# A two-layer encoder: q's head norm applied as a per-partition scale in the exponentials, and weight roundings queued behind PSUM evictions

## The chip, the cores and the metric

One Trainium2 chip; the kernel runs on one core. The metric is the device time of one execution in microseconds (us). A core has a matrix engine (PE, or TensorE), three engines for elementwise work (DVE, or VectorE; ACT, or ScalarE; POOL, or GpSimd) and SP, which in this kernel issues the DMAs. Each engine has its own instruction queue; they wait for each other by semaphores. Matmul results go to PSUM, and an engine reads them from there ("evicts" them) into SBUF, where the operands lie.

## The reference

Two layers over a sequence of 512 tokens of width 1024, then a last RMS norm. Cut to what the change touches:

```python
def gqa(h):                                   # 8 query heads, 2 key/value heads, width 64
    g_q = rope(rms_norm(g_q, q_norm))         # norm over each head's 64 values, then rotary
    g_k = rope(rms_norm(g_k, k_norm))
    for block of 128 queries:
        p = softmax(g_q @ g_k.T * 64 ** -0.5)
        o = p @ g_v

for l in range(2):
    h = rms_norm(x, norm_mix[l])
    x = x + concat([neighbourhood_attention(h), gqa(h)]) @ w_out[l]
    x = x + memory_cross_attention(rms_norm(x, norm_mem_q[l]), rms_norm(mem, norm_mem_kv[l]))
    x = x + conv_ffn(rms_norm(x, norm_ffn[l]))     # up, depthwise conv, silu(gate) * value, down
return rms_norm(x, norm_final)
```

Neighbourhood attention (NA) has 8 heads of width 64 over a window of the token grid; memory attention has 4 heads of width 128 over 256 memory tokens. All data are float32.

## The kernel before

**Products in three terms.** Every operand of a matmul is split into a rounded high part and the remainder, `hi` and `lo`, and a product is the sum of hi x hi, hi x lo and lo x hi. Activations lie transposed: features on the 128 partitions, tokens along the free axis.

**Weights.** `plan` lists all weight tiles in the order of their use. `emit_raw` loads one by DMA; `emit_split` (L245) rounds it: the high part is a copy on ACT (L265), the low part a subtraction on POOL (L266), in two halves for most weights. `get_w` (L269) is called where a weight is first used, and emits the roundings of the next two at that point. There are two raw buffers and four pairs of rounded ones. Outside the FFN the roundings are given a later place by priority (`behind(W_BEHIND)`).

**Order on the engines.** PE and SP run in the order of the program. On ACT, DVE and POOL a scheduler orders by priority; `behind(n)` moves an instruction back by n places, a negative n forward. `late(n, fn)` puts a step off by n ticks of the loop, so that a chain of small steps is spread between matmuls. `weave` runs attention stages over units one after the other and calls a filler, `attn_fill`, between them, which supplies matmuls of the projections until a given amount is used up. `attn_fill.step(n)` (L1029) takes n filler steps ahead of NA's weave: 3 in layer 0, 8 in layer 1.

**PSUM.** Three kinds of tiles: `ps_mm` (4 buffers, projections and products), `ps_s` (2, attention scores), `ps_t` (2, transpositions and statistics).

**First projections.** In layer 0 `project_first` (L604) works on the first three blocks q0, k0, q1 at once, as the input arrives; `project_qk` (L630) does one block, in two halves; `project_v` the values. `split_q` (L679) and `split_k` (L661) evict a block: a high copy on ACT and a subtraction on DVE for each of two heads (L682 and L684 for q). `split_psum` (L470) is the same for other tiles (L472 ACT, L473 DVE; with a scale L475 and L476).

**GQA's q and k.** `gqa_rope` (L835) takes each of q's four groups and k through steps one or two ticks apart. At the projection's end: two ACT readings of PSUM, the gained copy (L840) and the square (L841), and DVE's product with the cosines (L842). `swap`: four DMAs exchange partitions, eight small matmuls with `pairs` sum the squares per head (L850, into a `ps_t` tile), DVE divides and adds (L852, L855). `rotate`: POOL takes the power -1/2 (L862), copies it along each head's rows (L863), and does two passes of the rotation (L864, L865). `norm`: four matmuls on the identity turn the rows into a PSUM tile; one tick on, DVE multiplies the rotated tile into it (L875), and the split reads that.

**GQA's scores and softmax.** Per layer 16 units of 128 queries and two heads (j). `gqa_scores` (L889): matmuls into two score tiles, for each j the negated row maximum on DVE (L900) and the exponential with row sums on ACT (L902); then a reciprocal (L908), a per-partition multiply on POOL (`normalise`, L479), transposition and values. `mem_scores` (L1069) is memory attention's: the row maxima of two blocks in one instruction (L1076), their product with the query norms `mq.rstd`, 128x2 by 128x2 (L1077), and two exponentials whose scale is `mq.rstd` (L1081).

**The end.** `down_last` (L1225) adds the last products into x by chunks; ACT multiplies each by the final gain (L1241), while the squares go to the statistic; L1251 on DVE and L1249 on POOL multiply by the norm, and the result is stored.

Of the kernel before, what the change touches and what calls it, by code (L numbers as in the profile page):

```python
# [18 lines left out]
P = 128  # L19
# [5 lines left out]
NB = S // P  # L25
# [27 lines left out]
W_BEHIND, N_RAW, N_W, AHEAD, AHEAD_HELD, N_WARM, N_LATE, N_FIRST = 45, 2, 4, 2, 5, 8, 4, 3  # L53
# [120 lines left out]
def encoder_kernel(ctx: ExitStack, tc: tile.TileContext, t: dict, out: bass.AP):  # L174
# [60 lines left out]

    def raw_tile():
# [13 lines left out]
    def emit_split(act=ACT, cuts=2):  # L250
# [11 lines left out]
        with behind(W_BEHIND if done[0] and key[0] not in ("up", "down") else 0):  # L262
            for i in range(cuts):
                k = slice(nk * i // cuts, nk * (i + 1) // cuts)
                act.copy(hi[:, k], raw[:, k])  # L265
                (POOL if eng[0] == "P" else DVE).tensor_sub(lo[:, k], raw[:, k], f(hi)[:, k])  # L266
# [203 lines left out]
    def split_psum(hi, lo, ps, scale=None):  # L470
        if scale is None:
            ACT.copy(hi, ps)  # L472
            DVE.tensor_sub(lo, ps, f(hi))  # L473
        else:
            ACT.mul(hi, ps, scale)  # L475
# [56 lines left out]
    mem_rep = cpool.tile([P, MEMN], F32, name="mem_rep")  # L532

# [55 lines left out]
    for l in range(DEPTH):  # L589
# [41 lines left out]
        def project_qk(n, p):  # L631
            w = get_w((n, p))
            pm = ps_mm()
# [27 lines left out]
        def split_k(pm, kt, near):  # L661
            rows = [(slice(64 * j, 64 * j + 64), slice(64 - 64 * j, 128 - 64 * j)) for j in range(2)]
            for k, (r, o) in zip(kt, rows):
                ACT.copy(k[r, 0], pm[r])
                if near:
                    ACT.copy(k[o, 0], pm[r])
# [168 lines left out]
        def gqa_rope(g, pm):  # L835

            gain = qkg[:, l, 0:1] if g != "k" else qkg[:, l, 1:2]
            xs, sq, cc = tmp(), tmp(), tmp()
            with behind(-20):
                ACT.activation(xs, pm, AF.Copy, scale=gain)  # L840
                ACT.activation(sq, pm, AF.Square)  # L841
                DVE.scalar_tensor_tensor(cc, pm, gain, gtab[0][:, 0], op0=ALU.mult, op1=ALU.mult)  # L842

            def swap():
# [3 lines left out]
                pv = ps_t()  # L848
# [9 lines left out]
            def rotate(xr, v):  # L858
                r = small(2 * NB)
                rows = tmp()  # L860
                with behind(-40):
                    POOL.tensor_tensor(r, v, mhalf[:, : 2 * NB], op=ALU.pow)  # L862
                    POOL.tensor_copy(rows.rearrange("p (b d) -> p b d", d=HD), r.unsqueeze(2).to_broadcast([P, 2 * NB, HD]))  # L863
                POOL.tensor_mul(xr, xr, gtab[0][:, 1])  # L864
                POOL.tensor_add(xr, cc, xr)  # L865
                late(2, lambda: norm(xr, rows))

            def norm(xr, rows):
# [3 lines left out]
                late(1, lambda: split(xr, pr))  # L872

            def split(xr, pr):
                DVE.tensor_mul(pr, xr, pr)  # L875
                if g == "k":
                    gk.extend(rtile((2, S)) for _ in range(2))
                    split_k(pr, gk, False)
                else:
                    gq[g] = rtile((2, S))  # L880
                    split_q(pr, gq[g])
# [6 lines left out]
        def gqa_scores(u):  # L888
# [9 lines left out]
            for j in range(2):  # L898
                c = slice(j, j + 1)
                DVE.tensor_reduce(nmx[:, c], sc[j], axis=AX.X, op=ALU.max, negate=True)  # L900
                e = tmp()
                ACT.activation(e, sc[j], AF.Exp, bias=nmx[:, c], accum_out=sums[:, c])  # L902
# [126 lines left out]
        attn_fill.step(N_FIRST if l == 0 else N_FIRST + 5)  # L1029
# [39 lines left out]
        def mem_scores(u):  # L1069
# [7 lines left out]
            DVE.tensor_mul(nmx, nmx, mq.rstd[:, 2 * bp : 2 * bp + 2])  # L1077
# [154 lines left out]
        def down_last(g):  # L1232
# [144 lines left out]
```

## Time and profile before

| | |
|---|---|
| runs | 1391.63 us median of 3 (1390.44, 1391.63, 1395.34) |
| profiled execution | 1393.77 us, of which the span of the records is 1392.0 |
| mean granted TensorE clock | 0.994 |
| NA, layer 0 (with the start) / layer 1 | 0 to 140 / 703 to 824 us |
| GQA | 140 to 240 / 824 to 922 |
| memory attention | 240 to 327 / 922 to 1009 |
| FFN | 327 to 703 / 1009 to 1392 |

The stage limits are read from the timeline and rounded to a us. In the rows of the profile, `L265 ACT CAST hi<-raw 128x512` is an instruction of line 265 on ACT that writes tile `hi` from `raw`; `x2` counts instructions that a row puts together. In timeline rows the first two numbers are the start and the time that the row covers, and the bracket is the engine's idle time ahead of it and the instruction that ended it. DVE and ACT rows show the tiles they read and write, so a row `mm<-t,mm` reads and writes a projection's PSUM buffer.

### The profile page before, as it was taken

To read this page: it belongs to the slowest core of one execution; us is meant where nothing else is said; L and a number is where in the kernel's file an instruction comes from. 1 tells how busy PE (TensorE), PEld (TensorE's weight loads), DVE (VectorE), ACT (ScalarE), POOL (GpSimd) and SP (SyncE) were. 2 spreads that over 40 slices of the span, in tenths; PEclk is the share of its full clock that TensorE was granted. 3 is DMA by queue.
4 is the path that set the end of the run, shared out by engine and by line. 5 is a ranking of instruction groups with operands and counts; after the bars stand their busy time and mean duration, and the time that the engine had idled before them with its cause. 6 is when DMAs were issued, how large, how long until landed. Compare 5 with 4: busy or idle time off the path is not lost.

```text
span 1392.0 us, 19198 instructions
## 1 busy us (share of the span) xinstructions
PE 1354.7 (97%) x7072; PEld 1157.8 (83%) x7072; DVE 834.8 (60%) x1430; ACT 711.8 (51%) x1321; POOL 719.3 (52%) x537
## 2 busy tenths in 40 slices
PE   8999899999999999999999989999999999999997
PEld 7897789877888888888888978998788888888897
DVE  6666766364787177357446556754638843871873
ACT  6676577655443134234557656766554422432453
POOL 2458776635444444444645677756264444444441
PEclk9999999999999999999999999999999999999999
DMA  7653312422333333333356523223133333333331
GB/s 214 185 145 96 87 46 66 116 63 61 98 100 103 94 91 97 101 94 94 105 147 169 139 72 95 65 71 112 40 98 97 101 91 97 98 93 106 90 93 61
DMA packets 218205, 138.83 MB, mean 100 GB/s; under 512 B 6016, under 2 KB 211072, under 8 KB 218112
## 3 DMA queue, kind: packets, MB, share of 16 engines
q1 hardware_dynamic: 217968, 137.60, 34.6%
q8 instruction: 56, 0.92, 0.3%
q14 instruction: 37, 0.30, 0.1%
q10 hardware_dynamic: 144, 0.00, 0.0%
HBM read 125.00 MB, written 2.10 MB: 91 GB/s over the span
## 4 chain that ended last, share of the span: by engine, by line
PE 89%; DVE 4%; ACT 4%; issue 1%; DMA 1%; POOL 0%; DVEq 0%; ACTq 0%; SPq 0%
PE mm L77 82%; PE sc L77 4%; PE tr L64 3%; PE tr L77 1%; ACT hi L265 1%; DVE r L473 1%; DMA raw<-in_w_in 1%; ACT t L745 1%; DVE s L900 1%; DVE s L1077 1%; DVE xg L473 0%; DVE t L842 0%; ACT t L841 0%; ACT t L840 0%; ACT xg L438 0%
## 5 line engine op out<-in xcount | busy, mean ns | idle before, releaser
L266 POOL TENSOR_TENSOR lo<-raw,hi 128x1024 fp32r<-128x1024 f32 (+2 forms) x268 | 499.0, 1874 | 496.9 <-ACT hi L265 468.9
L77 PE MATMUL mm<-xg,hi 128*128 128x512 f32 x1984 | 617.7, 393 | 3.1 <-DVE t L842 2.9
L77 PEld LDWEIGHTS mm<-xg,hi 128*128 128x128 f32 x1984 | 370.4, 189 | 78.9 <-DVE t L842 3.3
L265 ACT CAST hi<-raw 128x512 fp32r<-128x512 f32 (+2 forms) x276 | 224.6, 837 | 346.7 <-PE mm L77 292.9
L77 PE MATMUL mm<-xg,lo 128*128 128x512 f32 x992 | 387.3, 391 | 0.0
L77 PE MATMUL mm<-r,hi 128*128 128x512 f32 (+1 forms) x1144 | 331.6, 374 | 2.3 <-ACT t L444 2.2
L77 PEld LDWEIGHTS mm<-r,hi 128*128 128x128 f32 x1144 | 207.3, 188 | 39.7 <-ACT t L444 3.1
L1201 DVE SCALAR_TENSOR_TENSOR t<-t,par,t 128x7 f32<-128x7 f32 (+1 forms) x352 | 201.9, 641 | 34.0 <-ACT t L1194 34.0
L77 PEld LDWEIGHTS mm<-xg,lo 128*128 128x128 f32 x992 | 187.1, 189 | 39.6
L77 PE MATMUL mm<-r,lo 128*128 128x512 f32 (+1 forms) x572 | 213.4, 373 | 0.0
L77 PEld LDWEIGHTS mm<-r,lo 128*128 128x128 f32 x572 | 108.0, 189 | 19.0
L1186 DVE TENSOR_TENSOR t<-mm,rep 128x512 f32<-128x512 f32 x88 | 60.1, 687 | 78.2 <-PE mm L77 62.1
L479 POOL TENSOR_SCALAR t<-t,s 128x512 f32<-128x512 f32 (+1 forms) x112 | 66.3, 608 | 75.4 <-DVE s L908 35.4
L1203 ACT ACTIVATE t<-t 128x512 f32<-128x512 f32 x44 | 27.8, 633 | 134.8 <-DVE t L1201 134.7
L1207 DVE TENSOR_TENSOR r<-t,r 128x512 fp32r<-128x512 f32 x44 | 90.5, 2056 | 7.4 <-ACT r L1206 4.3
L1230 DVE TENSOR_TENSOR xT<-xT,mm 128x512 f32<-128x512 f32 x32 | 21.9, 685 | 106.8 <-PE mm L77 106.8
L64 PE MATMUL tr<-ident,t 128*128 128x128 f32 x456 | 63.2, 275 | 13.3 <-DVE r L473 3.8
L77 PE MATMUL sc<-r,r 128*128 128x256 f32 (+1 forms) x352 | 72.6, 338 | 3.5 <-DVE r L473 2.5
L64 PEld LDWEIGHTS tr<-ident,t 128*128 128x128 f32 x456 | 52.4, 141 | 22.9 <-issue 9.7
L1194 ACT ACTIVATE t<-t,par 128x512 f32<-128x512 f32 x88 | 66.8, 806 | 3.2 <-DVE t L1186 3.2
L77 PE MATMUL mm<-r,r 128*128 128x256 f32 (+1 forms) x428 | 61.8, 297 | 0.0
L77 PEld LDWEIGHTS sc<-r,r 128*128 128x128 f32 x352 | 52.1, 192 | 8.3 <-DVE r L473 3.0
(145 smaller groups left out, 1554.1 us busy)
## 6 DMA issues: line engine op xcount, KB each, us to landing
raw<-in_w_up SPq DMA_DIRECT2D x88, 512.0 KB, 3.9
raw<-in_w_in SPq DMA_DIRECT2D x33, 512.0 KB, 4.5
raw<-in_w_down SPq DMA_DIRECT2D x32, 448.0 KB, 3.9
raw<-in_w_mem_kv SPq DMA_DIRECT2D x16, 512.0 KB, 4.0
raw<-in_w_down SPq DMA_DIRECT2D x16, 512.0 KB, 4.2
r<-in_bias SPq DMA_DIRECT2D x16, 384.0 KB, 5.8
r<-r SPq DMA_DIRECT2D x22, 256.0 KB, 5.2
raw<-in_w_out SPq DMA_DIRECT2D x8, 512.0 KB, 3.8
```

The source lines that it names most:

```text
L64: return lambda *a, **k: self.tc.keep_in_program_order(op(*a, **k))
L77: return self.tc.keep_in_program_order(self.engine.matmul(out, lhsT, rhs, **k))
L265: act.copy(hi[:, k], raw[:, k])
L266: (POOL if eng[0] == "P" else DVE).tensor_sub(lo[:, k], raw[:, k], f(hi)[:, k])
L473: DVE.tensor_sub(lo, ps, f(hi))
L479: eng.tensor_scalar(e, e, sums[:, col : col + 1], 1.0, op0=ALU.mult, op1=ALU.mult)
L1186: DVE.tensor_mul(u, us[side], ffn.rep)
L1194: ACT.activation(cc, u, AF.Identity, bias=par[:, l, CB + ch : CB + ch + 1], scale=w[1])
L1201: DVE.scalar_tensor_tensor(cc[:, dst], u[:, src], wi, cc[:, dst], op0=ALU.mult, op1=ALU.add)
L1203: ACT.activation(cs[0], cs[0], AF.Silu)
L1207: DVE.tensor_sub(acts[j][1], cs[0], f(acts[j][0]))
L1230: DVE.tensor_add(xT[m], xT[m], pm)
```

## The change

- `emit_split`: outside the FFN each high copy of a weight is ordered behind the last PSUM evictions on ACT that the program has written so far. Two are remembered in `evicted`: "projection" (`split_k`, `split_q`, the square of `gqa_rope`) and "other" (`split_psum`).
- `N_FIRST` 4 in place of 3; layer 1 still takes 8 steps.
- Layer 0's first two blocks (q0, k0) use `ps_s` tiles; in layer 1 `project_qk` does so for p = 0.
- `gqa_rope`: the pair statistics go to a `ps_mm` tile. For q the power is written to a lasting tile `qr[g]`; the copy along the rows, the identity matmuls and the multiply are left out, and the split reads the rotated SBUF tile one tick after the rotation. k keeps the old way.
- `gqa_scores`: the negated maximum is multiplied by q's norm (DVE, 128x1), and the exponential's scale is that norm.
- `mem_scores`: one 128x2 multiply becomes two per-partition multiplies of 128x1.
- `down_last`: the final gain is applied on DVE.

```diff
-W_BEHIND, N_RAW, N_W, AHEAD, AHEAD_HELD, N_WARM, N_LATE, N_FIRST = 45, 2, 4, 2, 5, 8, 4, 3
+W_BEHIND, N_RAW, N_W, AHEAD, AHEAD_HELD, N_WARM, N_LATE, N_FIRST = 45, 2, 4, 2, 5, 8, 4, 4
...
-        with behind(W_BEHIND if done[0] and key[0] not in ("up", "down") else 0):
+        ffn = key[0] in ("up", "down")
+        with behind(W_BEHIND if done[0] and not ffn else 0):
             for i in range(cuts):
                 k = slice(nk * i // cuts, nk * (i + 1) // cuts)
-                act.copy(hi[:, k], raw[:, k])
+                with ExitStack() as after:
+                    for e in evicted.values() if not ffn else ():
+                        after.enter_context(tc.issue_after(e))
+                    act.copy(hi[:, k], raw[:, k])
                 (POOL if eng[0] == "P" else DVE).tensor_sub(lo[:, k], raw[:, k], f(hi)[:, k])
...
-            ACT.copy(hi, ps)
+            evicted["other"] = ACT.copy(hi, ps).ins
...
+    qr = [cpool.tile([P, 2 * NB], F32, name=f"qr{i}") for i in range(4)]
...
-                    w[u], pms[u] = get_w(NA_ORDER[u]), ps_mm()
+                    w[u], pms[u] = get_w(NA_ORDER[u]), ps_s() if u < 2 else ps_mm()
...
-            pm = ps_mm()
+            pm = ps_mm() if p else ps_s()
...
             for v, r, o in halves:
-                ACT.copy(v[r], pm[r])
+                evicted["projection"] = ACT.copy(v[r], pm[r]).ins
...
-                pv = ps_t()
+                pv = ps_mm()
...
             def rotate(xr, v):
-                r = small(2 * NB)
-                rows = tmp()
+                r = small(2 * NB) if g == "k" else qr[g]
                 with behind(-40):
                     POOL.tensor_tensor(r, v, mhalf[:, : 2 * NB], op=ALU.pow)
-                    POOL.tensor_copy(rows.rearrange("p (b d) -> p b d", d=HD), r.unsqueeze(2).to_broadcast([P, 2 * NB, HD]))
+                if g == "k":
+                    rows = tmp()
+                    with behind(-40):
+                        POOL.tensor_copy(rows.rearrange("p (b d) -> p b d", d=HD), r.unsqueeze(2).to_broadcast([P, 2 * NB, HD]))
                 POOL.tensor_mul(xr, xr, gtab[0][:, 1])
                 POOL.tensor_add(xr, cc, xr)
-                late(2, lambda: norm(xr, rows))
+                if g == "k":
+                    late(2, lambda: norm(xr, rows))
+                else:
+                    late(1, lambda: split(xr))
...
+                r = 2 * b + j
                 DVE.tensor_reduce(nmx[:, c], sc[j], axis=AX.X, op=ALU.max, negate=True)
+                normalise(nmx[:, c], qr[i], r)
                 e = tmp()
-                ACT.activation(e, sc[j], AF.Exp, bias=nmx[:, c], accum_out=sums[:, c])
+                ACT.activation(e, sc[j], AF.Exp, bias=nmx[:, c], scale=qr[i][:, r : r + 1], accum_out=sums[:, c])
...
-        attn_fill.step(N_FIRST if l == 0 else N_FIRST + 5)
+        attn_fill.step(N_FIRST if l == 0 else N_FIRST + 4)
...
-            DVE.tensor_mul(nmx, nmx, mq.rstd[:, 2 * bp : 2 * bp + 2])
+            for i in range(2):
+                normalise(nmx[:, i : i + 1], mq.rstd, 2 * bp + i)
...
-                with behind(20):
-                    ACT.activation(xc, xc, AF.Copy, scale=gfin[:, m : m + 1])
+                DVE.tensor_scalar(xc, xc, gfin[:, m : m + 1], 1.0, op0=ALU.mult, op1=ALU.mult)
```

`normalise(e, sums, col, eng=DVE)` is unchanged: a `tensor_scalar` that multiplies e by one column of `sums`, one value to each partition (L479).

More of the change, by code (lines that the diff above doesn't have):

```diff
@@ L234, in encoder_kernel @@
     done = [0]
+    evicted = {}
     def raw_tile():
@@ L663, in split_k @@
             for k, (r, o) in zip(kt, rows):
-                ACT.copy(k[r, 0], pm[r])
+                e = ACT.copy(k[r, 0], pm[r])
                 if near:
-                    ACT.copy(k[o, 0], pm[r])
+                    e = ACT.copy(k[o, 0], pm[r])
+            evicted["projection"] = e.ins
             for k, (r, o) in zip(kt, rows):
```

16 lines of the change are left out of this document (9 added, 7 removed).

## The prediction

> **What bounds the kernel now.** I read the engines' busy time first, then busy time by stage, and then the timeline of TensorE (PE) for every place where it stood idle.
>
> ```profile
> PE 1354.7 (97%) x7072; PEld 1157.8 (83%) x7072; DVE 834.8 (60%) x1430; ACT 711.8 (51%) x1321; POOL 719.3 (52%) x537
> ```
>
> PE is busy for 97% of the span and no other engine for more than 60%. So the time can shrink in two ways only: less matmul work, or shorter idle times of PE. By stage (start, end, then busy time of PE, weight loads, DVE, ACT, POOL, then granted clock, DMA share, GB/s):
>
> ```profile
> 39.00:140.00 101.00, 97.58 (x620) 87.45 (x619) 62.55 (x154) 67.10 (x162) 62.12 (x66) 1.00 0.53 144
> 140.00:240.00 100.00, 93.61 (x602) 83.11 (x601) 69.43 (x128) 69.05 (x160) 70.39 (x83) 0.98 0.23 67
> 240.00:327.00 87.00, 83.33 (x443) 70.39 (x441) 46.76 (x92) 51.75 (x106) 42.68 (x27) 1.00 0.26 74
> 327.00:703.00 376.00, 375.99 (x1670) 311.72 (x1671) 222.25 (x309) 153.15 (x208) 180.85 (x88) 1.00 0.34 100
> 824.00:922.00 98.00, 94.03 (x601) 84.40 (x601) 65.44 (x125) 68.09 (x159) 69.92 (x83) 0.97 0.24 69
> 836.00:842.00 6.00, 6.00 (x25) 5.13 (x25) 2.66 (x7) 1.78 (x5) 6.00 (x8) 0.72 0.76 224
> ```
>
> The FFN (327 to 703) is full: 375.99 of 376 us, and nothing in this change can shorten it. The first layer's neighbourhood attention (to 140), GQA (to 240) and memory attention (to 327) leave PE idle for 3.4, 6.4 and 3.7 us; the second layer runs the same stages again (its GQA is the row from 824). In the last row PE's granted clock is 0.72 on average; I come back to it.
>
> These are the idle times that the change can reach (start, duration, and in brackets PE's idle time before it and what ended it):
>
> ```profile
> 34.84 0.35 PE L77 MATMUL mm<-hi,xg 128*128 128x256 f32 x1 [1.51 <-DVE r L684]
> 120.09 0.73 PE L77 MATMUL mm<-xg,hi 128*128 128x512 f32 x2 [1.44 <-DVE t L842]
> 138.67 0.63 PE L64 MATMUL tr<-ident,t 128*128 128x128 f32 x4 [1.91 <-DVE r L473]
> 148.91 1.05 PE L77 MATMUL tr<-pairs,t 128*128 128x2 f32 x8 [1.33 <-ACT t L841]
> 163.79 0.63 PE L64 MATMUL tr<-ident,t 128*128 128x128 f32 x4 [1.68 <-POOL r L524]
> 289.29 0.70 PE L64 MATMUL tr<-ident,t 128*128 128x128 f32 x4 [0.76 <-DVE t L479]
> 305.69 0.74 PE L77 MATMUL sc<-r,r 128*128 128x256 f32 x4 [1.27 <-DVE r L473]
> 823.15 0.99 PE L64 MATMUL tr<-ident,t 128*128 128x128 f32 x4 [1.91 <-DVE r L473]
> 834.96 1.05 PE L77 MATMUL tr<-pairs,t 128*128 128x2 f32 x8 [1.33 <-ACT t L841]
> 849.83 0.63 PE L64 MATMUL tr<-ident,t 128*128 128x128 f32 x4 [1.67 <-DVE xg L473]
> ```
>
> The second layer repeats the waits of 120, 289 and 305; its first stage has none like that of 34.84.
>
> **The change part by part.** Gains are minus.
>
> *Norm matmuls on the identity.* Each q group has four, eight rows in the trace:
>
> ```profile
> 127.51 1.05 PE L77 MATMUL mm<-ident,t 128*128 128x128 f32 x8
> 128.32 0.71 PE L77 MATMUL mm<-xg,hi 128*128 128x512 f32 x2
> ```
>
> Start to start that is 0.81 us of PE. Four q groups in two layers lose it: 8 x 0.81 = 6.5. In layer 1 one of them stands ahead of the wait at 823.15, whose chain does not get shorter (q's two ACT copies take the place of a rounding), so its 0.8 is only turned into waiting. I take 7 x 0.81 = -5.7; bounds 0 (all eaten by later waits) and -6.5. POOL's copy and DVE's multiply of the same groups leave too; they are off PE's path.
>
> *Weight roundings behind evictions.*
>
> ```profile
> 117.03 1.14 ACT L265 CAST hi<-raw 128x512 fp32r<-128x512 f32 x2
> 118.07 0.70 ACT L840 ACTIVATE t<-mm,qkg 128x512 f32<-128x512 f32 x1
> 118.64 0.61 ACT L841 ACTIVATE t<-mm 128x512 f32<-128x512 f32 x1
> 119.29 0.75 DVE L842 SCALAR_TENSOR_TENSOR t<-mm,qkg,r 128x512 f32<-128x512 f32 x1 [0.78 <-ACT t L841]
> ```
>
> Two halves of a rounding (1.14) run directly ahead of L840 and L841, and DVE's L842 frees the buffer for which PE stands idle for 1.44 at 120.09. Behind the change L840 and L841 stand first, so the chain ends 1.1 earlier: -1.1 in each layer, -2.2 together; bounds 0 and -2.9. What is late next is the rounded weight. At that place it is the first out projection's: subtraction on POOL from 118.82, first use at 149.82.
>
> ```profile
> 118.82 2.51 POOL L266 TENSOR_TENSOR lo<-raw,hi 128x512 fp32r<-128x512 f32 x2
> 149.82 0.71 PE L77 MATMUL mm<-r,hi 128*128 128x512 f32 x2
> ACT hi L265 <- PE mm L77: 292.9, 104, 5.9
> ```
>
> It is done at 121.3, 28 us early. The last row (all waits of that kind: us, times, longest) says that roundings mostly wait until PE releases a weight buffer, not for ACT. So I cost the delay at nothing; without that cover it would be up to one eviction, 1.3 (L840 and L841), per weight.
>
> *Score banks for the first two blocks, and N_FIRST 4.* The wait of 1.51 at 34.84 is for one of four projection buffers, which q0's eviction (L684) held. q0 and k0 now sit in the two score banks, idle until the first scores, so I take it as gone: -1.5, bounds 0 and -1.5. The extra filler step puts the value blocks ahead of the first scores: the same matmuls in another order, 0. The pair statistics take projection buffers instead of transposition ones: ten short uses, cost 0, bound +1.5 (one wait like that of 34.84).
>
> *The turn from NA to GQA.* With one filler step more, layer 0 does not have the three transpositions at 138.67 right behind one another; the wait of 1.91 goes: -1.9, bounds 0 and -1.9. Later in the same turn, the new order puts q3's second half, its pair statistics, the last NA values, the first scores and the out projection behind one another. The last third of that projection needs the last head group's low part from POOL, which is queued behind L862's power and three passes of q2 and q3 (L864, L865, one row quoted of each kind):
>
> ```profile
> L862 POOL TENSOR_TENSOR s<-s,mhalf 128x8 f32<-128x8 f32 x5 | 8.2, 1648 | 3.2 <-DVE s L855 3.1
> L865 POOL TENSOR_TENSOR t<-t,t 128x512 f32<-128x512 f32 x5 | 6.4, 1286 | 0.1
> ```
>
> With the subtraction itself at the 1.29 of L865, of the same shape, that is 1.65 + 4 x 1.29 = 6.8 us of POOL. PE has four scores and eight products to do meanwhile, at the pace of the FFN row (376 / 1670 = 0.225) 2.7, and eight values of half that width, 0.9: a new wait of 3.2, bounds 0 and 5. Against it goes the wait of 163.79 (1.68), while that of 148.91 stays in substance: 3.2 - 1.7 = +1.5. In layer 1 the order stays as it is, and the rounding ahead of 834.96 and the norms leave the chain: of 1.33 + 1.67 I count -1.7, bounds 0 and -3.0.
>
> The spell of lower clock in the stage table follows the wait of 834.96. It loses 6 x (1 - 0.72) = 1.7 us; the means of 0.98 and 0.97 over the two GQA stages are one and two such spells. Of two equal waits, 138.67 and 823.15, only the second is in a stage with two spells, so the trace does not say which wait brings one on: 0, bounds -5.1 (all three go) and +1.7. [...]
>
> *Per-partition norms in the memory attention.* L1077 multiplies 128x2 by a 128x2 tile, both in SBUF:
>
> ```profile
> L1077 DVE TENSOR_TENSOR s<-s,s x16: 140/150/1917, 285.9 to 992.5; 128x2 f32<-128x2 f32 x16
> 302.64 2.38 POOL L266 TENSOR_TENSOR lo<-raw,hi 128x1024 fp32r<-128x1024 f32 x1 [7.18 <-ACT hi L265]
> 303.13 1.91 DVE L1077 TENSOR_TENSOR s<-s,s 128x2 f32<-128x2 f32 x1
> L479 DVE TENSOR_SCALAR t<-t,s x32: 343/348/356, 288.9 to 994.5; 128x256 f32<-128x256 f32 x32
> 293.06 2.40 POOL L266 TENSOR_TENSOR lo<-raw,hi 128x1024 fp32r<-128x1024 f32 x1 [5.73 <-ACT hi L265]
> 295.27 0.61 DVE L479 TENSOR_SCALAR t<-t,s 128x256 f32<-128x256 f32 x2
> 113.35 0.55 DVE L855 TENSOR_SCALAR s<-s 128x8 f32<-128x8 f32 x1
> 112.60 1.28 POOL L266 TENSOR_TENSOR lo<-raw,hi 128x512 fp32r<-128x512 f32 x1
> ```
>
> Normally 0.15, it took 1.91 at 303.13 and ended when POOL's subtraction did (302.64 + 2.38). Behind it waited the eviction that ends PE's 1.27 at 305.69. A per-partition multiply of 128x256 (L479) kept its 0.34 to 0.36 in all 32 cases, one pair of them starting under POOL at 295.27. The new instruction is of that form with one column. So both waits go in each layer: 2 x (0.76 + 1.27) = -4.1, bounds 0 and -4.1. Against this speaks L855, a multiply by constants of 128x8: 0.55 under POOL at 112.60, ending with it.
>
> [...]
>
> *Norms in GQA's exponentials.* 64 multiplies of 128x1 come in, at 0.15 (L1077 undisturbed, the nearest in size) 0.3 per unit, ahead of the second exponential:
>
> ```profile
> 191.32 0.69 ACT L902 ACTIVATE t<-sc,s 128x512 f32<-128x512 f32 x1 [0.36 <-DVE s L900]
> 192.48 1.17 PE L77 MATMUL sc<-r,r 128*128 128x512 f32 x4
> ```
>
> It ends at 192.0; the next unit's scores start at 192.48 and overwrite that bank only in their second half, about 193.0. The 0.3 fits: 0, bounds 0 and +9.6 (32 units).
>
> *q's split from SBUF.* L684's 16 twins for GQA now read two SBUF tiles, as L1207 does:
>
> ```profile
> L1207 DVE TENSOR_TENSOR r<-t,r x44: 680/2414/2474, 365.3 to 1347.9; 128x512 fp32r<-128x512 f32 x44
> ```
>
> 0.69 becomes 2.4 where POOL runs a pass of 2.4. In GQA POOL is 70% busy with passes of mostly 1.3: a mean hold of 0.7 x 0.65 = 0.45, 7 us of DVE in all, of which I put a fifth on PE's path: +1.5, bounds 0 and +7.
>
> *Final scaling.*
>
> ```profile
> 1383.70 0.16 DVE L400 TENSOR_SCALAR s<-tr 128x2 f32<-128x2 f32 x1 [1.37 <-PE tr L77]
> ```
>
> On DVE it costs about 0.35 (L479) and falls into the 1.37 that DVE idles: 0.
>
> **Sum:** -5.7 - 2.2 - 1.5 - 1.9 + 1.5 - 1.7 - 4.1 + 1.5 = -14.1. The profiled execution took 1393.77 (span 1392.0), which is 2.1 above the median of the runs, so a profile of the changed kernel should show a span near 1377.9; against the median 1391.63 the forecast is 1377.5.
>
> **Rivals.**
> *(A) The waits form anew.* PE's queue has a fixed order, so a wait removed at one place can come back at the next, as at 823.15. Then only matmul work and half of the memory waits go: -5.7 - 2.0 + 1.5 = -6.2, 1385.4. For it speaks the new wait in the turn; against it, that the stage of memory attention has its waits far apart.
> *(B) The new DVE work is held by POOL.* If 128x1 multiplies behave like L855, each is held 0.45 on average; a unit's chain grows by 0.3 + 0.9 against 0.5 to 1.0 of slack (192.0 to 192.48 or 193.0), so 0.2 to 0.7, or 0.45 x 32 = 14, and the memory gain of 4.1 is lost: 1377.5 + 18 = 1395.5, no change that can be told. [...] L479's rows speak against it.
> *(C) Slower: the roundings arrive late.* 84 weight tiles outside the FFN (42 a layer by the plan) now queue behind evictions, which themselves wait for PE. It decides where a weight's lead is used up: from a mean lateness above 14.1 / 84 = 0.17 each the kernel is slower than before; with 0.35 it is +29, that is 1407. The lead of 28 us speaks against it in the turn; the start, where weights come straight from DMA, is less covered.
> *(D) The ordering does not bind:* the 2.2 is missing, 1379.4.
>
> **How the numbers follow.** Forecast with D, 1367 to 1383: 0.62. A, 1383 to 1389: 0.22. B: 0.09. C: 0.07. The low end is the sum without the new wait (-3.2) and with the three half-clock spells gone (-5.1), near 1369, and the rounding outwards; the high end takes in A with all holds of q's split (+3): 1389. Range 1367 to 1389, leaving out B and C. A measurement of this kernel tells 0.3% (4.2 us) from no change; faster means below 1387.5: all of the first, most of A, 0.83. Within: the rest of A and most of B, 0.10. Slower: 0.07.
>
> **What would show it.** In the changed kernel's profile: no identity matmuls between projections for q, PE busy shorter by about 6; L1077's successors at 0.15 throughout (held: B); no rounding between a projection's end and L840, and no PE wait on a rounded weight (there: C); no wait at the value blocks; one new wait on POOL's L500 twin in layer 0's turn; PE idle in both memory stages shorter by 2. The prediction is wrong if PE's idle time in GQA grows by more than 5 us per layer, or if the FFN's stage changes at all.

## The result and the profile after

The changed kernel takes 1414.66 us (median of 4 runs, 1411.81 to 1418.07) against 1393.41 for the kernel before on the same chip: a ratio of 1.0157, 95% interval 1.0129 to 1.0184. The forecast was 1377.5 and a gain. It is 21 us slower.

The busy times of the engines and the core's span and clock, after:

```profile
PE 1361.1 (96%) x7008; PEld 1154.0 (82%) x7008; DVE 848.4 (60%) x1518; ACT 708.1 (50%) x1305; POOL 719.0 (51%) x529
```

```profile
core 0: 1411.8 us, clock 0.988
```

The 64 rows of q's identity matmuls are gone (7072 to 7008), yet PE is busy for 6.4 us more than before. Its idle time is 1411.8 - 1361.1 = 50.7 us against 1392.0 - 1354.7 = 37.3. The mean granted clock fell from 0.994 to 0.988 (0.99434 and 0.98843 in the traces): what is missing to 1, times the span, is 7.9 us lost to the lower clock before and 16.3 after. The losses further on are worked out in the same way, from the unrounded clocks.

Where it went, by landmarks that every kernel of this study has. The times are read from the timelines; a stage runs from the landmark above to its own. "First FFN product" is DVE's first product of an up projection with the norm (L1186 before). e9, e6 and e13 are experiments below: the ordering alone, q's norm alone, and the change without these two.

| stage up to | before | after | e9 | e6 | e13 |
|---|---|---|---|---|---|
| first NA score, layer 0 | 37.8 | 38.8 | 36.6 | 37.1 | 39.1 |
| first GQA score | 108.7 | 107.2 | 113.9 | 108.5 | 105.0 |
| last GQA score | 84.4 | 98.9 | 85.1 | 91.7 | 84.2 |
| first FFN product | 123.8 | 119.8 | 124.8 | 126.5 | 121.2 |
| first NA score, layer 1 | 368.1 | 367.9 | 368.2 | 368.3 | 368.2 |
| first GQA score | 109.8 | 113.2 | 115.6 | 111.8 | 107.8 |
| last GQA score | 79.9 | 84.8 | 84.1 | 86.6 | 79.9 |
| first FFN product | 124.0 | 124.0 | 125.1 | 126.5 | 121.6 |
| end | 355.6 | 357.3 | 356.6 | 357.6 | 356.6 |

The FFN of layer 0 kept its time, as it should. GQA of layer 0 grew by 14.5 us, and layer 1's NA and GQA by 3.4 and 4.9. Some of TensorE's longest waits after, in the same columns as the prediction's:

```profile
132.36 0.63 PE L64 MATMUL tr<-ident,t 128*128 128x128 f32 x4 [1.98 <-DVE r L480]
144.00 1.05 PE L77 MATMUL mm<-pairs,t 128*128 128x2 f32 x8 [1.26 <-ACT t L851]
152.05 0.49 PE L77 MATMUL mm<-r,hi 128*128 128x512 f32 x1 [2.97 <-ACT r L506]
154.31 0.80 PE L77 MATMUL mm<-r,hi 128*128 128x512 f32 x1 [1.77 <-POOL r L507]
171.16 2.47 PE L77 MATMUL sc<-r,r 128*128 128x512 f32 x4 [4.36 <-ACT t L923]
290.30 1.05 PE L77 MATMUL tr<-ones,t 128*128 128x1 f32 x8 [1.59 <-DVE t L462]
815.35 0.70 PE L77 MATMUL mm<-xg,hi 128*128 128x512 f32 x2 [2.63 <-DVE r L677]
836.30 0.96 PE L64 MATMUL tr<-ident,t 128*128 128x128 f32 x4 [4.01 <-DVE r L480]
```

The waits at 34.84, 163.79 and 849.83, and those of L1077 in the memory stages, are gone. The wait on the out projection's last operand that the prediction foresaw is there: 2.97 + 1.77. Those of 132.36, 171.16, 815.35 and 836.30 were not foreseen. That of 171.16 is followed back here (ACT, POOL and the DMA queue of SP, from their timelines):

```profile
153.94 2.18 ACT L272 CAST hi<-raw 128x512 fp32r<-128x512 f32 x4
...
156.43 5.04 POOL L273 TENSOR_TENSOR lo<-raw,hi 128x512 fp32r<-128x512 f32 x4
...
158.99 2.88 SPq L64 DMA_DIRECT2D raw<-in_w_mem_kv  x2
161.92 1.12 SPq L64 DMA_DIRECT2D r<-in_memT  x2
...
167.10 1.06 ACT L548 ACTIVATE r<-r 128x1024 f32<-128x1024 f32 x1 [2.78 <-DMA r<-in_memT]
...
170.24 0.78 ACT L923 ACTIVATE t<-sc,s,qr 128x512 f32<-128x512 f32 x1
```

Two weights are rounded one behind the other, after the evictions, from 153.94 to 161.5. Their loads' successors in SP's queue come next, and memT stands behind them, issued at 161.92 (before: at 151.47). ACT's queue holds the squares of memT (L548) ahead of an exponential, and waits 2.78 us for the data. The exponential frees the score bank for which PE stands idle 4.36 us.

And the wait of 836.30, on POOL and ACT:

```profile
829.42 2.70 POOL L273 TENSOR_TENSOR lo<-raw,hi 128x512 fp32r<-128x512 f32 x2
832.08 1.26 POOL L877 TENSOR_TENSOR t<-t,t 128x512 f32<-128x512 f32 x1
...
833.38 1.26 ACT L691 CAST r<-t 64x512 fp32r<-64x512 f32 x2 [0.75 <-POOL t L877]
834.66 1.07 ACT L479 CAST r<-tr 128x512 fp32r<-128x512 f32 x2
```

Two POOL halves of a rounding (2.70) stand ahead of the rotation's last pass (L877). q's split (L691) reads what L877 writes, is at the head of ACT's queue, and keeps back the evictions of two transpositions (L479), for which PE waits. Before, the split read a PSUM tile and came later. This wait belongs to the norm and not to the ordering: without the ordering (e1 below) it is still 3.68.

### The profile page after: what moved, and what is told of

Read it like the earlier page. It is cut to its first block, busy times and chain, and to the rows that moved or that the text cites. A ratio compares the mean times of both kernels' runs of the same rounds, so it can differ in the third digit from the quotient of the medians.

```text
span 1411.8 us, 19071 instructions
## 1 busy us (share of the span) xinstructions
PE 1361.1 (96%) x7008; PEld 1154.0 (82%) x7008; DVE 848.4 (60%) x1518; ACT 708.1 (50%) x1305; POOL 719.0 (51%) x529
## 4 chain that ended last, share of the span: by engine, by line
PE 78%; POOL 6%; DMA 5%; DVE 3%; ACT 3%; issue 3%; SPq 1%; DVEq 0%; ACTq 0%; POOLq 0%
PE mm L77 70%; PE sc L77 5%; POOL lo L273 3%; PE tr L64 3%; DMA raw<-in_w_mem_q 1%; DMA t<-t 1%; PE tr L77 1%; SPq L64 1%; ACT hi L272 1%; DMA raw<-in_w_in 1%; POOL t L877 1%; DVE xg L480 1%; POOL t L486 1%; POOL t L462 1%; ACT t L923 0%
## 5 line engine op out<-in xcount | busy, mean ns | idle before, releaser
L273 POOL TENSOR_TENSOR lo<-raw,hi 128x1024 fp32r<-128x1024 f32 (+2 forms) x268 | 501.0, 1881 | 510.5 <-ACT hi L272 505.2
L77 PE MATMUL mm<-xg,hi 128*128 128x512 f32 x1920 | 598.5, 393 | 2.6 <-DVE r L677 2.6
L77 PEld LDWEIGHTS mm<-xg,hi 128*128 128x128 f32 x1920 | 359.7, 189 | 75.4 <-issue 2.8
L77 PE MATMUL mm<-xg,lo 128*128 128x512 f32 x960 | 375.9, 392 | 0.0
L77 PE MATMUL mm<-r,hi 128*128 128x512 f32 (+1 forms) x1144 | 335.8, 377 | 7.2 <-ACT r L506 3.0
L77 PEld LDWEIGHTS mm<-xg,lo 128*128 128x128 f32 x960 | 181.6, 189 | 38.5
L923 ACT ACTIVATE t<-sc,s,qr 128x512 f32<-128x512 f32 x64 | 49.4, 776 | 34.3 <-DVE s L486 34.2
```

Source lines behind the costliest of these rows:

```text
L77: return self.tc.keep_in_program_order(self.engine.matmul(out, lhsT, rhs, **k))
L923: ACT.activation(e, sc[j], AF.Exp, bias=nmx[:, c], scale=qr[i][:, r : r + 1], accum_out=sums[:, c])
```

## The experiments

The times of before are those of the runs beside each kernel. "Norm" is q's head norm in the exponentials, "ordering" that of roundings behind evictions.

| run | us | before | ratio (95% interval) |
|---|---|---|---|
| e1 after, without ordering | 1402.5 | 1391.8 | 1.0075 (1.0060 to 1.0090) |
| e2 after, split late | 1411.5 | 1391.8 | 1.0141 (1.0126 to 1.0156) |
| e3 after, without ordering, split late | 1403.1 | 1392.6 | 1.0076 (1.0060 to 1.0092) |
| e4 after, memT early | 1425.5 | 1391.8 | 1.0240 (1.0225 to 1.0255) |
| e5 after, 3 filler steps | 1409.1 | 1391.8 | 1.0121 (1.0105 to 1.0138) |
| e6 before + norm | 1416.0 | 1392.0 | 1.0169 (1.0154 to 1.0184) |
| e7 e6, split late | 1412.1 | 1392.0 | 1.0139 (1.0124 to 1.0155) |
| e8 before + memory norms, final gain | 1387.4 | 1392.0 | 0.9963 (0.9949 to 0.9977) |
| e9 before + ordering | 1411.1 | 1392.0 | 1.0134 (1.0118 to 1.0149) |
| e10 before + norms of one | 1398.8 | 1392.4 | 1.0047 (1.0032 to 1.0062) |
| e11 e6 without the multiplies | 1404.3 | 1392.4 | 1.0084 (1.0067 to 1.0102) |
| e12 e8 + score banks | 1390.1 | 1392.4 | 0.9980 (0.9970 to 0.9990) |
| e13 after, without ordering, without norm | 1385.4 | 1392.4 | 0.9948 (0.9931 to 0.9965) |
| e15 e13 + ordering behind the square | 1397.0 | 1392.6 | 1.0036 (1.0021 to 1.0051) |
| e16 before, split from SBUF alone | 1397.0 | 1392.6 | 1.0033 (1.0020 to 1.0046) |
| e17 e16, split late | 1398.5 | 1392.6 | 1.0044 (1.0028 to 1.0060) |
| e18 e11, budget as before | 1396.6 | 1392.3 | 1.0024 (1.0014 to 1.0035) |
| e19 e1, budget as before | 1403.6 | 1392.3 | 1.0074 (1.0047 to 1.0102) |

### What undoing one part of the changed kernel gives

e1 takes the ordering out:

```diff
-                    for e in evicted.values() if not ffn else ():
+                    for e in ():
```

> The changed kernel with weight roundings free again (no ordering behind evictions), all else as changed. Theory O (the ordering is the cause: late roundings keep both raw buffers full, so the load of memT stands in SP's queue behind a weight load that waits for a buffer, and ACT's squares of memT, L548, hold up the exponentials for the 4.36 us of TensorE idle at 171.16): the idle at 171.16 goes with its half-clock spell, about -6, and in layer 1 the wait of 4.01 at 836.30 shrinks by a POOL rounding pass of 2.7; 1405 to 1408. Theory S (q's earlier split makes ACT wait for POOL's rotation): within 3 us of the changed kernel's 1414.7, the waits at 152 and 836 stay. Theory N (the extra filler step): within 3 us as well.

1402.5: 12 us less than the changed kernel, more than its theory had. The wait of 171.16 is gone and that of 815.35 is 1.37; that of 836.30, which should have shrunk by 2.7, is 3.68. Taking out the ordering gives back more than half of the loss, and the rest stands without it.

e2 puts the split where it stood:

```diff
-                    late(1, lambda: split(xr))
+                    late(3, lambda: split(xr))
```

> The changed kernel with q's split three ticks after the rotation instead of one, which is where it stood before. Theory S: ACT no longer stands at the split (L691) waiting for POOL's rotation (L877), so the waits on L506 at 152.05 (2.97) and on L480 at 836.30 (4.01) fall to below 2 each, about -5 in all: 1408 to 1411. Theory O or N: no more than 2 us, 1412 to 1416, and the idle of 4.36 at 171.16 stays.

3 us less. The wait of 836 fell from 4.0 to 1.9, but that on L506 in layer 0 grew from 2.97 to 3.80. The place of the split is not the main cause.

e4 issues memT's loads earlier:

```diff
-MEM_STEPS = [0, 0, 1, 0, 1, 1, 1, 1, 1, 1, 1] + [0] * 9
+MEM_STEPS = [1, 0, 0, 0, 1, 1, 1, 1, 1, 1, 1] + [0] * 9
```

> The changed kernel with memT's two loads issued four units earlier, ahead of the two weight loads that they stood behind; nothing else is moved. If the idle of 4.36 us at 171.16 is due to memT landing late, it goes with the half clock behind it: -4 to -7, 1408 to 1411. If it is ACT's order in itself (L548 ahead of the exponentials), it stays above 3 us and the time stays at 1413 to 1416.

Both expectations missed: it is 11 us slower. TensorE in e4:

```profile
152.03 0.61 PE L77 MATMUL mm<-r,hi 128*128 128x512 f32 x1 [4.37 <-ACT r L506]
156.60 0.80 PE L77 MATMUL mm<-r,hi 128*128 128x512 f32 x1 [3.96 <-POOL r L507]
171.49 0.73 PE L77 MATMUL sc<-r,r 128*128 128x512 f32 x2 [1.01 <-ACT t L923]
```

The wait that it was made for fell from 4.36 to 1.01. But POOL now took two multiplies ahead of L507, and of the two waits ahead of it the first grew from 2.97 to 4.37 and the second from 1.77 to 3.96; layer 1, in which memT's load moved too, lost more. The late load was a true link of one wait and not a cause that could be taken out by itself.

e5 takes back the extra filler step:

```diff
-N_LATE, N_FIRST = 45, 2, 4, 2, 5, 8, 4, 4
+N_LATE, N_FIRST = 45, 2, 4, 2, 5, 8, 4, 3
```

> The changed kernel with 3 filler steps ahead of the first weave, as before the change; layer 1 unchanged with 8. Theory N (the extra step is the cause: memT behind a second weight load, and the turn's order in layer 0): layer 0's GQA stage loses most of its 12 us of added idle, -8 to -12: 1403 to 1407, with the waits of layer 1 unchanged. Theory O: -2 to +2, since the roundings are still late; memT, whose loads stand ahead again, decides between them: if only it mattered, -4 to -7.

5.6 us less: layer 0's GQA gave back 11.7 and the first stage 3.5, and the stage between them took 9.3. That is the range forecast if only memT mattered, which e4 contradicts, so e5 does not decide between the theories.

### The parts alone, on the kernel before

e6 has q's norm in the exponentials alone (the hunks of the change in `gqa_rope` and `gqa_scores`, with the statistic left in `ps_t`), e7 the same with the split three ticks on; e8 the hunks in `mem_scores` and `down_last`; e9 the ordering with its `evicted` entries, and nothing else. Their cores:

```diff
 e6
+                normalise(nmx[:, c], qr[i], r)
+                ACT.activation(e, sc[j], AF.Exp, bias=nmx[:, c], scale=qr[i][:, r : r + 1], accum_out=sums[:, c])
...
+                    late(1, lambda: split(xr))
 e7
-                    late(1, lambda: split(xr))
+                    late(3, lambda: split(xr))
 e8
-            DVE.tensor_mul(nmx, nmx, mq.rstd[:, 2 * bp : 2 * bp + 2])
+            for i in range(2):
+                normalise(nmx[:, i : i + 1], mq.rstd, 2 * bp + i)
 e9
+                    for e in evicted.values() if key[0] not in ("up", "down") else ():
+                        after.enter_context(tc.issue_after(e))
```

> The kernel before with one part of the change alone: q's head norm in the exponentials (no identity matmuls for q, split from SBUF one tick after the rotation, two 128x1 norms a unit). Theory P (the prediction's term: seven times 0.81 of matmul time is won): 1385 to 1388. Theory S (the early split makes ACT wait for POOL's rotation, and both row maxima are taken ahead of both norms, so the first exponential is late): the 6.5 us of matmuls come back as waits in GQA, 1391 to 1397.

> As e6_qnorm_on_before, with q's split three ticks after the rotation, where it stood. Theory S: the wait of the third transposition (138.67 and 823.15 before, 1.91 each) is no longer than before, and the run is 3 to 5 us below e6; 1387 to 1391. If instead the two row maxima ahead of the norms are what costs, it is within 1 us of e6.

> The kernel before with only the per-partition norms in the memory attention and the final gain on DVE. Theory P: the two waits a layer behind L1077 (0.76 and 1.27) go, -4.1, and the gain costs nothing: 1387 to 1388.5. Rival (the new multiplies are held by POOL like L855, or the eviction behind them waits for something else just as long): 1391 to 1393.

> The kernel before with only the ordering of weight roundings behind evictions. Theory P: the 1.44 at 120 and its twin shrink by 1.1 each, 1389 to 1391. Theory O (late roundings, as the -12 of e1_no_order against the changed kernel say): slower than before by some of those 12, 1396 to 1404. If it comes out under 1393, the 12 us are not the ordering's own but arise with q's early split or with the extra filler step.

e6 is 24 us slower and e9 19, both beyond every range given; each by itself costs about as much as the whole change. e7 is 4 us below e6, as Theory S had it, but the wait at the third transposition is still 2.9 in both layers (1.91 before), and the run is 20 us slower than before: the tick is a small part. e8 gains 4.6, where 4.1 was forecast. In e8 the new multiplies read:

```profile
L479 DVE TENSOR_SCALAR s<-s,s x32: 202/205/215, 286.5 to 986.7; 128x1 f32<-128x1 f32 x32
```

All 32 took 202 to 215 ns. Eight of them started under a POOL subtraction with 1.2 to 1.9 us left, and none was held as L1077 was (1472 to 1917 ns at its four starts under a POOL subtraction, before).

e9 shows the ordering at its plainest, for TensorE's and SP's instructions stand in the order of before, one by one. ACT and PE in e9:

```profile
117.69 1.17 ACT L668 CAST r<-mm 64x512 fp32r<-64x512 f32 x2 [5.68 <-DVE mm L880]
...
120.25 0.69 ACT L845 ACTIVATE t<-mm,qkg 128x512 f32<-128x512 f32 x1
...
120.45 0.70 PE L77 MATMUL mm<-xg,hi 128*128 128x512 f32 x2 [2.63 <-DVE r L673]
162.31 1.00 PE L77 MATMUL mm<-ident,t 128*128 128x128 f32 x4 [3.23 <-POOL t L868]
```

k's split (L668) now stands ahead of NA's exponentials and of L845 (before L840) on ACT, which idles 5.68 us for it. The wait at 120, which the ordering was to shorten from 1.44, is 2.63. And the identity matmul of 162.31 waits 3.23 for POOL's copy, in whose queue two moved halves of a rounding (2.53) stand further ahead.

e15 orders behind the square of `gqa_rope` alone, on e13, the instruction for which the prediction had counted its gain; this is the only entry in `evicted`:

```diff
+                evicted["projection"] = ACT.activation(sq, pm, AF.Square).ins
```

> e13_no_order_no_qnorm with the roundings ordered behind the last square of gqa_rope alone, not behind the splits. The prediction's term (1.44 at 120 shrinks by 1.1 in layer 1, where e13 still has 1.53 at 799): 1383 to 1385. If any such ordering disturbs ACT's queue as e9 did, 1389 or more.

It is 12 us slower than e13, as its second theory had it. PE in e13, then PE and POOL in e15:

```profile
799.02 0.50 PE L77 MATMUL mm<-xg,hi 128*128 128x512 f32 x1 [1.38 <-DVE t L842]
```

```profile
806.74 0.74 PE L77 MATMUL mm<-xg,hi 128*128 128x512 f32 x2 [0.56 <-DVE t L846]
...
836.62 3.79 POOL L270 TENSOR_TENSOR lo<-raw,hi 128x512 fp32r<-128x512 f32 x3
...
845.75 0.64 POOL L867 COPY t<-s 128x512 f32<-128x512 f32 x1
846.44 1.44 PE L77 MATMUL mm<-ident,t 128*128 128x128 f32 x5 [3.75 <-POOL t L867]
```

The gain is there: 1.38 falls to 0.56. So is its price: four POOL halves of roundings, run together (three of them 3.79), push the chain of the next group back, and PE waits 3.75 for its last copy.

### What in q's norm costs

e10 keeps q's old way and multiplies by one in the softmax; e11 has e6's q path but no multiplies in the softmax, so that q's norm is left out:

```diff
+                normalise(nmx[:, c], ones, 0)
-                ACT.activation(e, sc[j], AF.Exp, bias=nmx[:, c], accum_out=sums[:, c])
+                ACT.activation(e, sc[j], AF.Exp, bias=nmx[:, c], scale=ones[:, 0:1], accum_out=sums[:, c])
```

> The kernel before with two multiplies by one (128x1, DVE) and a scale of one read per partition in each GQA unit: TensorE's order and every result are those of the kernel before, only the softmax chain is longer. Theory X (the longer chain, 2 x 0.2 on DVE, about 0.08 more on each exponential and both maxima ahead of both norms, is what costs in e6_qnorm_on_before): half or more of its 24 us, 1402 to 1412. Rival S (q's split behind POOL's rotation costs it): 1392 to 1396, the chain fits between the units.

> e6_qnorm_on_before without the two multiplies and without the scale in the exponentials (q's head norm is left out of the computation); TensorE's order and q's split are e6's. Theory S: 1408 to 1416, since the split in front of ACT's queue stays; the waits of 3.5 at the third transposition (137.79 and 834.52 in e6) stay. Theory X: 1388 to 1398.

6.5 and 12 us, each between the ranges given: both count, and together they make 18 of e6's 24. The groups of exponentials in the kernel before and in e10:

```profile
L902 ACT ACTIVATE t<-sc,s 128x512 f32<-128x512 f32 x64 | 44.1, 693 | 19.2 <-DVE s L900 18.7 <-DVE s L548 0.4
```

```profile
L903 ACT ACTIVATE t<-sc,s,ones 128x512 f32<-128x512 f32 x64 | 49.6, 778 | 31.2 <-DVE s L479 31.0
```

A scale read per partition makes each exponential 85 ns longer, and ACT's idle time ahead of them grows from 19.2 to 31.2 us. The price of the scale could be read before; NA's exponentials have a constant scale, the memory attention's one per partition:

```profile
L745 ACT ACTIVATE t<-sc,s 128x256 f32<-128x256 f32 x64 | 29.5, 473 | 25.1 <-DVE s L739 25.0
L1081 ACT ACTIVATE t<-sc,s,s 128x256 f32<-128x256 f32 x32 | 17.8, 562 | 15.5 <-DVE s L1077 15.5
```

The longer idle time goes with DVE's order; in the changed kernel:

```profile
159.77 1.28 DVE L920 TENSOR_REDUCE s<-sc 128x1 f32<-128x512 f32 x2
160.97 0.33 DVE L486 TENSOR_SCALAR s<-s,qr 128x1 f32<-128x1 f32 x2
```

Both maxima come ahead of both multiplies, in 28 of the 32 units here and in 27 of e10's, so the first exponential waits for the second maximum as well (0.6 more) and no longer overlaps it. How the 6.5 us divide between the two was not tested.

e16 moves q's split to SBUF but leaves the identity matmuls in place on another tile, unused, so that TensorE's order is that of before; e17 has the split at its old tick. e18 takes the matmuls out and charges their time to the filler's budget all the same:

```diff
+                    def credit():
+                        PE.ns += 4 * 107.0
+
+                    late(2, credit)
```

e16 and e17 have this in its place:

```diff
+                    def unused():
+                        pr = ps_mm()
+                        for b in range(NB):
+                            PE.matmul(pr[:, b * P : (b + 1) * P], cc[:, b * P : (b + 1) * P], ident, start=True, stop=True)
+
+                    late(2, unused)
```

> The kernel before with q's split taken from SBUF one tick after the rotation; the identity matmuls stay on TensorE in their places with an unused result, and q's head norm is left out of the computation, so TensorE's order is that of before. Theory S (the split waits for POOL in ACT's queue): most of e11's +12, 1399 to 1405, with the wait at the third transposition above 3. Theory F (the missing matmuls move the filler's work): within 3 us of before, 1390 to 1395.

> e16_split_only with the split three ticks after the rotation. Theory S: the loss of e16 shrinks by 4 or more, 1391 to 1398. If it stays within 1.5 us of e16, it is not the tick but the reading of SBUF (both inputs of DVE's subtraction in SBUF, held by POOL).

> e11_no_norm with the identity matmuls' time still charged to the filler's budget: TensorE's order is that of before with the eight groups taken out, nothing else is moved; q's head norm is left out of the computation. Theory F (the new order of the matmuls is what costs): e16's 1397.0 less 5.7 to 6.5, 1390 to 1392. Rival W (the matmuls covered waits, which now show wherever they stand): 1396 to 1405.

e16 is 4.5 us slower than before, between its two ranges, and e17 5.9: the split from SBUF costs, at either tick. DVE's subtractions in e16, in e17, and in the changed kernel from SBUF and from PSUM:

```profile
L685 DVE TENSOR_TENSOR r<-t,r 64x512 fp32r<-64x512 f32 x16 | 12.3, 771 | 0.9 <-ACT r L683 0.4
L685 DVE TENSOR_TENSOR r<-t,r 64x512 fp32r<-64x512 f32 x16 | 18.0, 1124 | 1.1 <-ACT r L683 0.8
L693 DVE TENSOR_TENSOR r<-t,r 64x512 fp32r<-64x512 f32 x16 | 17.4, 1084 | 6.0 <-ACT r L691 5.6
L693 DVE TENSOR_TENSOR r<-mm,r 64x512 fp32r<-64x512 f32 x12 | 8.3, 689 | 5.0 <-ACT r L691 4.9
```

Against 689 ns from PSUM, the 16 are held for 1.3 us in all in e16 and for 7.0 in e17. So the hold that e17's second branch names is there, but e16 loses 4.5 almost without it. What the two share is ACT's order; in e16:

```profile
148.29 1.26 ACT L683 CAST r<-t 64x512 fp32r<-64x512 f32 x2
...
151.32 0.59 ACT L843 ACTIVATE t<-mm 128x512 f32<-128x512 f32 x1
151.97 1.67 PE L77 MATMUL tr<-pairs,t 128*128 128x2 f32 x8 [2.61 <-ACT t L843]
```

The split's two copies (L683) now stand ahead of the last group's square (L843), in e17 as well, and the wait for it, 1.33 in each layer before, is 2.61 in both layers of e16 and 2.99 and 2.66 in e17.

e18 should have been 6 us under e16, for it has those 64 rows of matmuls less in the same order. It is level with it (1396.6, 1397.0). PE in e16, then in e18:

```profile
139.15 1.09 PE L64 MATMUL tr<-ident,t 128*128 128x128 f32 x4 [2.68 <-DVE r L473]
826.41 0.63 PE L64 MATMUL tr<-ident,t 128*128 128x128 f32 x4 [1.90 <-DVE r L473]
```

```profile
139.21 1.09 PE L64 MATMUL tr<-ident,t 128*128 128x128 f32 x4 [4.13 <-DVE r L473]
825.46 1.09 PE L64 MATMUL tr<-ident,t 128*128 128x128 f32 x4 [3.87 <-DVE r L473]
```

In layer 0 the transposition comes at the same time with the matmuls and without, for in both the split's copies, ahead of its evictions on ACT, wait for POOL's rotation until 134.0 and 134.1. PE waits 1.5 us longer for it, and 2.0 in layer 1. In these two executions the lower clock lost 13.0 us in e16 (clock 0.9907) and 17.8 in e18 (0.9872). So the matmuls' time came back as waits and, here, as lower clock; that second part is less firm, since e18's ten runs had clocks from 0.987 to 0.992 and e16's six from 0.991 to 0.993. e11, in which the budget was not charged, is 7.7 us slower than e18, with nothing but TensorE's new order between them. On the changed kernel without the ordering, the same charge gave nothing:

> e1_no_order with the same charge, so TensorE's order is e13's without the eight groups. Theory F: e13's 1385.4, +6.5 for the softmax chain (e10), +4.5 for the split (e16), -5.7 for the matmuls: 1389 to 1393. Rival W: 1399 to 1404.

1403.6 against e1's 1402.5: rival W. Nor did the late split there:

> The changed kernel without the ordering and with q's split three ticks after the rotation. From e1 (-12) and the gain of the late split in e7 against e6 (-4): 1397 to 1400. If the softmax chain (6.5 in e10) is then all that is lost against e13's 1385.4, with the 5.7 of matmul time won, 1386 to 1392.

1403.1, as e1, above both ranges. With the matmuls at nothing, as e18 has them, the parts on top of e13 make 1385.4 + 6.5 + 4.5 = 1396.4; the other 7 us were not resolved.

### What is left when both are taken out

e12 adds the score banks for q0 and k0 to e8; e13 is the changed kernel without ordering and norm, that is e12 with the fourth filler step and the statistic in `ps_mm`:

```diff
 e12
+                    w[u], pms[u] = get_w(NA_ORDER[u]), ps_s() if u < 2 else ps_mm()
...
+            pm = ps_mm() if p else ps_s()
 e13
+N_LATE, N_FIRST = 45, 2, 4, 2, 5, 8, 4, 4
...
+                pv = ps_mm()
```

> e8_memnorm_gfin with q0 and k0 in the score banks as well, nothing else. If the projection buffer is what the wait at 34.5 (2.1) is for, it goes: 1385 to 1387. If the first scores then wait for the evictions of q0 and k0 just as long (as 0.8 and 1.4 at 36 to 38 in e5_first3), 1387 to 1389.

> The changed kernel without the ordering and without q's norm in the exponentials: what is left is the extra filler step, the score banks, the statistic in a projection buffer, the norms in the memory attention and the final gain. If the two parts that were taken out carry the whole loss, 1383 to 1389. If the extra step and the new buffers cost by themselves, above 1391; e5_first3 (the step undone: -5.6) speaks for some 1390 to 1394.

e12 is 1390.1, 1 us above its second branch: the first scores wait 1.30 and 1.14 us for the evictions of k0 in place of the 34.5 wait. With the fourth filler step, which puts the value blocks in between, e13 has neither, and with 1385.4 it is the lowest time here: 0.9948 of before (the interval of e8 overlaps its own).

## Why the prediction was wrong, by its steps

From e13 (0.9948) the norm leads to e1 (1.0075), and the ordering from there to the changed kernel (1.0157): -7, +18 and +11 us by the ratios. Alone on the kernel before, they cost 24 and 19, more than they add to e13. Part of that is plain: e9's waits of 3.23 (at 162.31) and of 3.80 in layer 1 are on identity matmuls that the norm takes out. The rest of it stays open.

The waits of weight roundings for PE, of which the prediction quotes the sum of 292.9, stand here for the two FFN stages of the kernel before alone (327 to 703 and 1009 to 1392):

```profile
ACT hi L265 <- PE mm L77: 134.2, 40, 5.9
ACT hi L265 <- PE mm L77: 121.2, 36, 5.9
```

- *Weight roundings, "-2.2", "I cost the delay at nothing".* This is the step that failed first. I looked for the next user of the rounded weight, for which PE waited 0.96 and 0.27 us in one value block of layer 0 and nowhere else in NA or GQA, and did not list what the moved roundings stand ahead of in their new place. The row of 292.9 us that was to show the cover was also read wrongly: 255.4 of them are the FFN's, where nothing is reordered. Outside it 28 of the 140 high copies waited for PE, 37.5 us in all. What the runs showed in its place: the ordering alone costs 19 us (e9), and taken out of the changed kernel it gives 12 back (e1). Rival C had the sign but not the mechanism: not a late weight, but k's split, POOL's copies of the norm and memT's load behind the roundings and evictions. The gain at the one place was real (e15: 1.38 to 0.56).
- *Identity matmuls, "-5.7".* e18 against e16: -0.5, no difference that can be told. I had seen that one group in front of a wait is worth nothing, and counted the other seven in full; the wait at the third transposition took back 1.5 us in layer 0 too. The bound of 0 was the right value. Their missing charge to the filler moved later matmuls too, 7.7 us in e11, a step that the prediction did not have.
- *Norms in GQA, "The 0.3 fits: 0".* e10: +6.5, inside the bound of +9.6. I had the multiplies right (0.33 per unit), and missed the longer exponential, whose price stood in the profile of before (L1081 against L745, 562 and 473 ns), and that a scheduler may put both maxima first.
- *q's split, "+1.5".* The term was mis-sized: e16 +4.5, within its bound of 7, and for another reason. DVE's hold was as forecast in the changed kernel (16 x 0.4 = 6.3 us, 7 estimated), but e16 has 1.3 us of it. The term left out the split's copies on ACT, which stand ahead of the square (L843 in e16) and, one tick after the rotation, wait for POOL.
- *Half clock, "0".* After, 8.4 us more were lost, against a bound of +1.7. Mean clock and span give 7.9 us lost before and 7.4 in e13, but 14.5 in e9, 16.3 after and 18.0 in e6.
- *The turn.* The "-1.9" did not come: the three transpositions no longer stand behind one another, but one of them waits 1.98 at 132.36. The new wait on the last operand was predicted at 3.2, for POOL's low part, and is 4.7, of which 2.97 is for the high copy on ACT (L506). In layer 1 the wait for the pair statistics fell to 0.36 and that of 849.83 went, as counted, but that of 823.15 (1.91) became one of 4.01.
- *Memory norms, -4.1; start, -1.5; final gain, 0.* Right: e8 -4.6, and the wait of 34.84 is gone. The choice between L479 and L855 had little behind it, though: at 295.27 POOL had only 0.19 us left (293.06 + 2.40); e8's eight rows under POOL decide it. The score banks pay only with the fourth filler step (e12 2.7 above e8, e13 2.1 below it, the last within the intervals). In the changed kernel layer 1's memory stage takes as long as before, since new waits came in there (1.63 at 978.72, the twin of 290.30, and 0.97 at 1011.16); layer 0's is 4.0 shorter.
- *Small sums.* Rival D's time should be 1377.5 + 2.2 = 1379.7, and the high end takes in +3 for q's split where its bound of 7 adds 5.5, which would have made it 1391. Neither reaches 1414.66.

Rival A (waits form anew) named part of the mechanism, but priced it at the gain's size: waits can come back longer than what was removed. B did not happen: the 96 new multiplies of 128x1 in the changed kernel took 193 to 216 ns, though 61 of them started while POOL was at work.

## What to carry to other kernels

On queues that run in order, a moved instruction has to be priced by everything that it now stands ahead of, on each engine it uses, and not by the user of its result alone. A row that sums a whole kernel can hide that its waits lie in another stage than the one that is changed. Work taken off a busy engine in front of a wait is no gain: ask what the engine waits for next, and whether that arrives earlier. Where a change has parts that can be had by themselves (here e8, and e13 at 0.9948), try the parts alone first.

## What the runs showed of the hardware

An exponential on ACT over 128x512 took 693 ns with a constant scale and 776 to 778 with one read per partition; over 128x256, 473 and 562. A DVE multiply of 128x2 with both inputs in SBUF took 140 to 152 ns, and 1472 to 1917 where it started under a POOL subtraction; a per-partition multiply of 128x1 took 193 to 216 in either case (33 of the changed kernel's 96 started under such a subtraction, L273).

PE's lower clock came with idle time, but not in step with it. With PE's idle time (span less busy time) ahead of the loss to the clock, both in us: before 37.3 and 7.9, e13 30.1 and 7.4, e10 41.7 and 7.1, e9 50.2 and 14.5, after 50.7 and 16.3. A stretch in the changed kernel, around the wait of 171.16, in the columns of the prediction's stage table:

```profile
168.00:172.00 4.00, 0.84 (x2) 0.50 (x2) 1.07 (x2) 3.66 (x8) 3.75 (x9) 0.86 0.00 0
172.00:176.00 4.00, 3.97 (x10) 2.82 (x10) 3.40 (x7) 3.17 (x9) 3.65 (x5) 0.50 0.00 0
176.00:180.00 4.00, 4.00 (x20) 3.30 (x19) 3.97 (x6) 1.22 (x4) 2.34 (x4) 0.79 0.47 127
```

The clock was 0.86, 0.50 and 0.79 in them. By single us it was 0.92 from 170 to 171, 0.50 in each of the six up to 177, and 0.66 in the next: 6.8 us at half clock, with an idle time of 4.36 ahead of 171.16. In the kernel before, behind the wait of 1.33 at 834.96, the five us from 836 to 841 had 0.96, 0.50, 0.50, 0.50 and 0.83: 3.4 us at half clock.
